# Second columns of the in-projection's norm turned by VectorE squares and one exchange, under three weight blocks summed over the first columns

## The chip, the cores and the metric

The kernel runs on one core of a Trainium2 chip. The metric is the device time of one execution in microseconds (us). A range of 0.2% of this kernel's time, 1.11 us, is about what a measurement can tell from no change.

## The reference

One layer of a decoder trunk on 256 tokens of width 1024, in float32:

```python
h = x + 0.5 * swiglu(rms_norm(x, g1), ...)              # FFN 1, hidden width 2816
u = rms_norm(h, mix_norm)
proj = u @ w_in                                         # 1024 x 5120
q_a, k_a, v_a, q_b, k_b, v_b, g_a, g_b = split(proj)    # 6 x 512, 2 x 1024
y_a = moba(rotary(q_a), rotary(k_a), v_a)               # 256 tokens: plain causal attention
y_b = stick_breaking(q_b, k_b, v_b)
h = h + (sigmoid(g_a) * (y_a @ w_a) + sigmoid(g_b) * (y_b @ w_b)) @ w_out
h = h + 0.5 * swiglu(rms_norm(h, g2), ...)              # FFN 2
out = rms_norm(h, final_norm)
```

## The kernel before

**Matmuls in three passes.** Every float32 operand is split into a high part (`wh`, `uh`, ...) and a rest (`wl`, `ul`, ...), and a product is three matmuls into one PSUM bank (lines 307, 308, 309): high by high, high by rest, rest by high. One `unit` is these three matmuls for one weight tile of 128 x 512 and one token half `t` (128 tokens).

**Weights.** A stream of 376 weight tiles comes from HBM in the order of use, two tiles (512 KB) to a DMA on SP's queue (line 154, `raw`). `Weights.split` makes `wh` on ScalarE (ACT) and `wl` on VectorE (DVE), lines 165/166, or 169/170 where the norm's gain is multiplied in. There are ten pairs of buffers (`WB = 10`): tile i+10 is split when tile i has been used by both token halves. Tiles 132 to 211 belong to the in-projection, eight tiles (the depth 1024 in pieces of 128) to each of ten column blocks of 512: 0 to 2 are q_a, k_a, v_a, 3 to 5 q_b, k_b, v_b, 6 to 9 the gates.

**Order of work.** The orders of TensorE (PE) and SP are written out by hand. `weave` is a list of generators: after every unit a `tick` lets those that are due issue their next step, with waits counted in ticks (the constants `D_...`). The orders of ScalarE, VectorE and GpSimd (POOL) are a scheduler's.

**Norms and turned operands.** The matmul wants the activations with the depth on the partitions. The row scale of the norm, `r` (`rms`), is applied later when a bank is read out; ScalarE takes the squares, VectorE two steps, POOL the Newton steps (lines 354, 360, 361). Columns are turned in one of three ways in `Normed`: `half` turns 512 columns of one token half by four TensorE transposes (line 375, bank `tp_u`) and a split; `moved` turns squares of 32 x 32 on VectorE (line 383) and then moves the squares between partitions by 16 DMAs of 16 KB within SBUF (`exchange`, line 460, half on SP, half on POOL); `moved_both` does that for both token halves with one exchange of 16 DMAs of 32 KB, tiles `zs` (squares) and `zm` (moved). The in-projection's norm (`u`) uses `moved` for the first 512 columns and `half` for the second. The norm of FFN 2 (`z`) uses `moved` for the first columns and `moved_both` for the second.

**FFN 2's start.** Since its second columns come late, `three_blocks` sums three weight blocks over the first columns first (24 units), and then the same three over the second columns (24 units). In the first 24 units token half 1 is 8 units behind half 0, in the second 24 it is 2 behind. Four of the six banks are two pairs of the pool `pr`, two are of the pool `acc`.

**In-projection before.** `project` sums one block over the whole depth: block 0 with half 1 eight units behind, the others two behind. `heads` runs q, k, v in that order; after q and k of the first attention (`rotary`) POOL rotates (`rotate`, lines 740 to 743), and ten ticks later (`D_TURN`) TensorE turns them (`qtpa`, `ktpa`, line 775). Two `lane` generators work through four pairs of heads of each attention, long steps between units of the in-projection: scores `S`, weights turned (`ptp`), values `y_a`; then `z`, its sums over later keys (lines 908 to 910) and `y_b`. What the lanes have not issued when the first columns of the first branch product (`ba`) are done is issued at once (`weave.flush(long=True)`).

Of the kernel before, what the change touches and what calls it, by code (L numbers as in the profile page):

```python
# [21 lines left out]
KD = D // P  # L22
# [8 lines left out]
W_IN = FB * KD + 2 * KF  # L31
# [8 lines left out]
D_TURNED = 3  # L40
# [4 lines left out]
D_TURN = 10  # L45
D_READY = 7
D_NORM = 4
# [3 lines left out]
D_PAIR = (6, 1)  # L51
# [146 lines left out]
def hybrid_layer_kernel(ctx, tc, x, xt, pos, g_final, bgate, wstream, out):  # L198
# [10 lines left out]
    def acc_bank(nm):  # L209
        return psum.tile([P, 512], F32, name=nm, tag="acc", bufs=3)  # L210
# [4 lines left out]
    def two_banks(nm):  # L215
        return psum.tile([P, 1024], F32, name=nm, tag="pr", bufs=2)
# [19 lines left out]
    def gain(i):  # L236
        for n, (lo, hi) in enumerate(((0, FB * KD), (W_IN, W_BR), (W_FFN2, W_FFN2 + FB * KD))):
            if lo <= i < hi:
                k = (i - lo) % KD
                if n == 0 and i < 2 * KD:  # L240
                    k = i // 2
                if n == 2 and i - lo < 3 * KD:
                    k = (i - lo) // 12 * 4 + (i - lo) % 4
                return gk[:, n * KD + k:n * KD + k + 1]
        return None
# [5 lines left out]
    def load_x(queue, k0, k1):  # L251
# [33 lines left out]
                            base=0, pattern=[[0, 4], [-1, P]], channel_multiplier=1)  # L285
# [3 lines left out]
                            base=0, pattern=[[-1, P]], channel_multiplier=1)  # L289
# [11 lines left out]
    weave = Weave()  # L301
# [110 lines left out]
    class Given(Normed):  # L412


        made = [big(f"x{q}{j}") for j in range(2) for q in "hl"]
# [16 lines left out]
    def later(f, *args):  # L432
        f(*args)
        return
        yield

    def lagged(n, lag):

        for k in range(n + lag):
            if k < n:  # L440
                yield 0, k
            if k >= lag:
                yield 1, k - lag
# [18 lines left out]
            if m % len(queues) == len(queues) - 1:  # L462
                yield gap

    def three_blocks(x, base, banks, evac):

        for c in range(2):
            for t, n in lagged(12, 2 if c else KD):
                b, k = divmod(n, 4)
                i = base + c * 12 + n  # L470
                unit(banks(t, b), x[t].blk(c * 4 + k), W.get(i), c == 0 and k == 0, c == 1 and k == 3)
                if t == 1:
                    W.done(i)
                if c == 1 and k == 3:
                    evac(b, t, banks(t, b))


    def ffn(base, xn, nm, on_half, lag, last=False):
# [27 lines left out]
        for b in range(FB):  # L506
            if b == 1:
                W.ahead = AHEAD
            if b == 3 and last:
                ordered.enter_context(tc.manual_schedule())  # L510
            banks = {}
            if b == 0 and lag == 0:
                pairs = [two_banks(f"gu_{nm}{c}") for c in range(2)]
                os = [[pair[:, t * 512:t * 512 + 512] for t in range(2)] for pair in pairs]
                for i in range(2 * KD):
                    k, c = divmod(i, 2)
                    blocks = [xn[t].blk(k) for t in range(2)]
                    if i == 0:
                        keep_warm(os[c], False)
                        unit_halves(os[c], blocks, W.get(base))  # L520
                    else:
                        unit_pair(os[c], blocks, W.get(base + i), k == 0, k == KD - 1)
                    W.done(base + i)

                for c in range(2):
                    for t in range(2):
                        weave.add(later(hidden, c, t, os[c][t]), D_GIVEN[c][t])
            if b == 0 and lag:
                gus = {}

                def gu_bank(t, b):
                    if (t, b) not in gus:
                        if b < 2:

                            pair = two_banks(f"gu_{nm}{b}")
                            gus[0, b], gus[1, b] = pair[:, 0:512], pair[:, 512:1024]
                        else:
                            gus[t, b] = acc_bank(f"gu_{nm}{b}_{t}")
                    return gus[t, b]

                three_blocks(xn, base, gu_bank, lambda b, t, ps: weave.add(later(hidden, b, t, ps), D_PAIR[t] if b < 2 else 0))
            for t, k in lagged(KD, 2) if b > (2 if lag else 1) else ():
                if k == 0:
                    banks[t] = acc_bank(f"gu_{nm}{b}_{t}")
                i = base + b * KD + k
                unit(banks[t], xn[t].blk(k), W.get(i), k == 0, k == KD - 1)
                if t == 1:
                    W.done(i)
                if k == KD - 1:
                    weave.add(later(hidden, b, t, banks[t]))  # L550

        base += FB * KD
        banks = {}
# [45 lines left out]
        for t, c in ((0, 0), (0, 1), (1, 0), (1, 1)) if last else ((0, 0), (1, 0), (0, 1), (1, 1)):  # L599
            pieces = (0, 1) if last and (t, c) == (1, 1) else (None,)  # L600
            for piece in pieces:
                for k in range(head, KF):
                    i = base + 2 * head + c * tail + k - head
# [7 lines left out]
    xn = [Given(t) for t in range(2)]  # L611
# [76 lines left out]
    un = [None, None]  # L688

    def next_norm(dst, nm):  # L690
        both = []

        def on_half(t, c, piece=None):
            def go():
                dst[t].half(c)
                dst[t].rms()
                return
                yield

            if c == 0:  # L700
                dst[t] = Normed(t, nm)
                weave.begin(dst[t].moved(c))
            elif nm == "z":
                weave.add(later(dst[t].rms), D_NORM)
                if t == 0:
                    both.append(Normed.moved_both(c, dst))
                    next(both[0])
                else:
                    weave.begin(both[0])
            else:  # L710
                weave.add(go(), D_NORM)

        return on_half

# [6 lines left out]

    def project(bi, evac):
        banks = {}
        for t, k in lagged(KD, KD if bi == 0 else 2):
            if k == 0:
                banks[t] = acc_bank(f"in{bi}_{t}")
            i = W_IN + bi * KD + k
            unit(banks[t], un[t].blk(k), W.get(i), k == 0, k == KD - 1)
            if t == 1:
                W.done(i)  # L730
            if k == KD - 1:
                evac(t, banks[t])
# [10 lines left out]
        marks["rot"] = g.tensor_add(d3[:, :, 0:16], t1, t2).ins  # L743

    def heads(b0, nm, res, rotary, diagonal):


        for j, which in enumerate("qk"):
# [17 lines left out]
            def turn(which=which, src=src, squares=squares):  # L766
                if rotary:
                    tp = two_banks(f"{which}tp{nm}")
                else:
                    tp = big(f"{which}m{nm}", F32)  # L770
                    yield from exchange(tp, squares, 8, [nc.sync, nc.gpsimd], 1)
                    yield D_LANDED
                for pr in range(4 if rotary else 0):
                    for t in range(2):
                        nc.tensor.transpose(tp[:, pr * 256 + t * P:pr * 256 + (t + 1) * P], src[t][:, pr * P:(pr + 1) * P], ident)
                if which != diagonal:
                    parts = big(f"{which}Th{nm}"), big(f"{which}Tl{nm}")
                    for c in range(2):
                        s = slice(c * 512, c * 512 + 512)
                        if rotary:  # L780
                            split(parts[0][:, s], parts[1][:, s], tp[:, s])
                        else:
                            split(plain(parts[0][:, s]), plain(parts[1][:, s]), slots(tp, 8)[:, c * 4:c * 4 + 4])
                            yield D_PIECE
                    ready = [[q[:, pr * 256:(pr + 1) * 256] for q in parts] for pr in range(4)]
                else:
                    tp4 = slots(tp, 8).rearrange("p (c t) g w -> p c t g w", t=2)
                    for c in range(2):
                        for j in range(2):
                            rows = slice(j * HD, j * HD + HD)  # L790
                            dst = [q[rows].rearrange("p (c j t g w) -> p c j t g w", c=2, j=2, t=2, g=4)[:, :, j] for q in res["bd"][c]]
                            split(dst[0], dst[1], tp4[rows, c * 2:c * 2 + 2])
                            yield D_PIECE
                    ready = [[q[:, pr % 2 * 512:pr % 2 * 512 + 512] for q in res["bd"][pr // 2]] for pr in range(4)]
                yield D_READY if rotary else D_READY - D_PIECE
                res[which] = ready

            if which == diagonal:
                res["bd"] = [(big(f"bdh{nm}{c}"), big(f"bdl{nm}{c}")) for c in range(2)]
                for c in range(2):  # L800
                    for q in res["bd"][c]:
                        for half in range(2):
                            q5 = q[half * HD:(half + 1) * HD].rearrange("p (c j t) -> p c j t", c=2, j=2)
                            nc.gpsimd.memset(q5[:, :, 1 - half, :].bitcast(F32), 0.0)
            project(b0 + j, evac)
            weave.add(turn(), D_TURN if rotary else D_TURNED)

        vs = big(f"vh{nm}"), big(f"vl{nm}")

# [5 lines left out]
            if t == 1:  # L815
                res["v"] = [[q[:, s * 512:(s + 1) * 512] for q in vs] for s in range(2)]

        project(b0 + 2, evac_v)

    def pass3(o, a, b, first, last):  # L820
        for i, (p, q) in enumerate(((0, 0), (0, 1), (1, 0))):
# [100 lines left out]
    a, b, ys = {}, {}, {}  # L922
# [52 lines left out]
    for c in range(2):  # L975
        banks = {}
# [156 lines left out]
```

## Time and profile before

| what | value |
|---|---|
| time, median of 3 runs | 554.25 us (554.15 to 554.33) |
| the profiled execution | 554.34 us, its span from first to last instruction 552.6 us |
| TensorE busy | 545.0 us, 99% of the span, 2490 instructions |
| VectorE, ScalarE, GpSimd busy | 400.6, 338.2 and 78.1 us |
| mean granted TensorE clock | 0.997 |
| DMA queue of SP (q1) | 108.16 MB, 61.3% of the 16 engines' span |

A busy TensorE says little by itself here: matmuls overlap (one of 128 x 512 lasts 0.39 us, and the next starts 0.227 us after it), so a delay is read from the starts, not from the busy time. The rows on which the argument rests stand in the prediction.

### The profile page before, as it was taken

Reading aid. Unit: us, or ns where it says so; the run is one execution under the profiler, and the core shown is the slowest. Engines: PE = TensorE matmul, PEld = TensorE weight load, DVE = VectorE, ACT = ScalarE, POOL = GpSimd, SP = SyncE. Lnnn points to the kernel's source line nnn. Section 1 sums busy time; section 2 is a strip of 40 time slices with the busy share of each in tenths; the row PEclk is TensorE's granted clock in tenths of the full one; section 3 lists DMA queues with packets and bytes.
Section 4 is the critical chain, followed back from the end, with each engine's and each line's share of the span. In section 5 each row is a group of like instructions: output and inputs, shape, how many; then the busy total and the mean of one; then the engine's idle time right before and its main releaser. Section 6 shows DMA issues by size and latency. Waiting matters only on the chain.

```text
span 552.6 us, 7886 instructions
## 1 busy us (share of the span) xinstructions
PE 545.0 (99%) x2490; PEld 449.4 (81%) x2490; DVE 400.6 (72%) x691; ACT 338.2 (61%) x578; POOL 78.1 (14%) x156
## 2 busy tenths in 40 slices
PE   9999999999999999999999999999999999999995
PEld 6888888888888888888888888887888888888884
DVE  5797788766566666889888888777776778655645
ACT  6865666655453767677875774466766566555533
POOL 1410000000003736022022200471000000000000
PEclk9999999999999999999999999999999999999998
DMA  8947776775774676455555464586768766757722
GB/s 283 406 136 238 231 218 206 224 242 180 229 243 157 197 237 213 155 160 182 173 154 175 139 197 151 180 263 215 226 187 251 228 206 210 227 172 246 240 69 76
DMA packets 43722, 112.22 MB, mean 203 GB/s; under 512 B 8352, under 2 KB 17568, under 8 KB 43680
## 3 DMA queue, kind: packets, MB, share of 16 engines
q1 hardware_dynamic: 40992, 108.16, 61.3%
q0 software_dynamic: 2256, 2.89, 2.0%
q10 hardware_dynamic: 432, 0.67, 0.3%
q8 instruction: 19, 0.31, 0.2%
q14 instruction: 23, 0.19, 0.1%
HBM read 102.25 MB, written 1.05 MB: 187 GB/s over the span
## 4 chain that ended last, share of the span: by engine, by line
PE 99%; ACT 0%; DVE 0%; issue 0%; ACTq 0%
PE gu_f L308 13%; PE gu_f L307 13%; PE gu_f L309 13%; PE dn_f L307 7%; PE dn_f L308 7%; PE dn_f L309 7%; PE in L307 7%; PE in L309 7%; PE in L308 7%; PE wo L309 1%; PE wo L307 1%; PE wo L308 1%; PE gu_f L320 1%; PE gu_f L321 1%; PE gu_f L323 1%; PE y_a L822 1%
## 5 line engine op out<-in xcount | busy, mean ns | idle before, releaser
L170 DVE SCALAR_TENSOR_TENSOR wl<-raw,first,wh 128x512 fp32r<-128x512 f32 (+1 forms) x257 | 182.0, 745 | 45.9 <-ACT wh L169 44.9
L169 ACT ACTIVATE wh<-raw,first 128x512 fp32r<-128x512 f32 (+1 forms) x257 | 172.5, 715 | 61.5 <-DMA raw<-in_wstream 34.9
L165 ACT CAST wh<-raw 128x512 fp32r<-128x512 f32 x120 | 70.5, 619 | 63.6 <-DMA raw<-in_wstream 36.0
L166 DVE TENSOR_TENSOR wl<-raw,wh 128x512 fp32r<-128x512 f32 x120 | 78.5, 689 | 39.7 <-ACT wh L165 39.2
L308 PE MATMUL gu_f<-wl,zh 128*128 128x512 f32 x176 | 68.6, 390 | 0.0
L307 PE MATMUL gu_f<-wh,zh 128*128 128x512 f32 x176 | 68.5, 389 | 0.0
L309 PE MATMUL gu_f<-wh,zl 128*128 128x512 f32 x176 | 68.5, 389 | 0.0
L307 PE MATMUL dn_f<-wh,hth_f 128*128 128x512 f32 x172 | 67.1, 390 | 0.0
L309 PE MATMUL dn_f<-wh,htl_f 128*128 128x512 f32 x172 | 66.9, 389 | 0.0
L308 PE MATMUL dn_f<-wl,hth_f 128*128 128x512 f32 x172 | 66.9, 389 | 0.0
L307 PE MATMUL in<-wh,uh 128*128 128x512 f32 x160 | 63.5, 397 | 0.0
L309 PE MATMUL in<-wh,ul 128*128 128x512 f32 x160 | 62.5, 391 | 0.0
L308 PE MATMUL in<-wl,uh 128*128 128x512 f32 x160 | 62.5, 390 | 0.0
L307 PE MATMUL gu_f<-wh,xh 128*128 128x512 f32 x144 | 56.0, 389 | 0.0
L308 PE MATMUL gu_f<-wl,xh 128*128 128x512 f32 x144 | 56.0, 389 | 0.0
L309 PE MATMUL gu_f<-wh,xl 128*128 128x512 f32 x144 | 56.0, 389 | 0.0
L308 PEld LDWEIGHTS gu_f<-wl,zh 128*128 128x128 f32 x176 | 33.0, 188 | 7.3 <-DVE wl L170 0.4
L307 PEld LDWEIGHTS gu_f<-wh,zh 128*128 128x128 f32 x176 | 33.0, 188 | 6.9
L309 PEld LDWEIGHTS gu_f<-wh,zl 128*128 128x128 f32 x176 | 33.0, 188 | 6.8
L307 PEld LDWEIGHTS dn_f<-wh,hth_f 128*128 128x128 f32 x172 | 32.3, 188 | 7.0 <-DVE sh_f L487 0.4
L309 PEld LDWEIGHTS dn_f<-wh,htl_f 128*128 128x128 f32 x172 | 32.3, 188 | 6.8
L308 PEld LDWEIGHTS dn_f<-wl,hth_f 128*128 128x128 f32 x172 | 32.3, 188 | 6.5
(251 smaller groups left out, 780.9 us busy)
## 6 DMA issues: line engine op xcount, KB each, us to landing
raw<-in_wstream SPq DMA_DIRECT2D x185, 512.0 KB, 4.3
hm_f<-hs_f SPq DMA_DIRECT2D x160, 32.0 KB, 3.9
raw<-in_wstream SPq DMA_DIRECT2D x5, 256.0 KB, 4.9
h<-in_x SPq DMA_DIRECT2D x2, 512.0 KB, 8.3
bg<-in_bgate POOLq DMA_DIRECT2D x4, 256.0 KB, 4.7
xin<-in_xt SPq DMA_DIRECT2D x2, 256.0 KB, 6.7
hm_f<-hs_f SPq DMA_DIRECT2D x32, 16.0 KB, 3.1
gB<-in_g_final POOLq DMA_DIRECT2D x1, 512.0 KB, 5.9
```

The costliest lines, as they stand in the source:

```text
L165: self.nc.scalar.copy(hi, raw)
L166: self.nc.vector.tensor_sub(lo, raw, hi.bitcast(F32))
L169: self.nc.scalar.activation(hi[:, s], raw[:, s], AF.Copy, scale=g)
L170: self.nc.vector.scalar_tensor_tensor(lo[:, s], raw[:, s], g, hi[:, s].bitcast(F32), op0=ALU.mult, op1=ALU.subtract)
L307: nc.tensor.matmul(o, ah, wh, start=first, stop=False)
L308: nc.tensor.matmul(o, ah, wl, start=False, stop=False)
L309: nc.tensor.matmul(o, al, wh, start=False, stop=last)
L320: nc.tensor.matmul(o, ah, wh, start=first, stop=False)
L321: nc.tensor.matmul(o, al, wh, start=False, stop=False)
L323: nc.tensor.matmul(o, ah, wl, start=False, stop=last)
L822: nc.tensor.matmul(o, a[p], b[q], start=first and i == 0, stop=last and i == 2, skip_group_check=True)
```

## The change

Norm `u` is now handled like norm `z`: its second columns are turned by `moved_both` (new tiles `us`, `um`), and blocks 0, 1 and 2 of the in-projection (q_a, k_a, v_a) run through `three_blocks`. The stream of weights is put in that order on the host, `gain` finds the right piece of the gain for it, and the banks' helper moves from `ffn` into `three_blocks`. The read-out of q_a, k_a and v_a and the turns of q_a and k_a now hang on the end of each block in the second 24 units.

```diff
-                if n == 2 and i - lo < 3 * KD:
+                if n > 0 and i - lo < 3 * KD:
                     k = (i - lo) // 12 * 4 + (i - lo) % 4
...
-    def three_blocks(x, base, banks, evac):
+    def three_blocks(x, base, nm, evac):
+        made = {}
+        def banks(t, b):
+            if (t, b) not in made:
+                if b < 2:
+                    pair = two_banks(f"{nm}{b}")
+                    made[0, b], made[1, b] = pair[:, 0:512], pair[:, 512:1024]
+                else:
+                    made[t, b] = acc_bank(f"{nm}{b}_{t}")
+            return made[t, b]
...
         def on_half(t, c, piece=None):
-            def go():
-                dst[t].half(c)
-                dst[t].rms()
-                return
-                yield
             if c == 0:
                 dst[t] = Normed(t, nm)
                 weave.begin(dst[t].moved(c))
-            elif nm == "z":
+            else:
                 weave.add(later(dst[t].rms), D_NORM)
                 if t == 0:
                     both.append(Normed.moved_both(c, dst))
                     next(both[0])
                 else:
                     weave.begin(both[0])
-            else:
-                weave.add(go(), D_NORM)
...
-        for t, k in lagged(KD, KD if bi == 0 else 2):
+        for t, k in lagged(KD, 2):
...
-            project(b0 + j, evac)
-            weave.add(turn(), D_TURN if rotary else D_TURNED)
+            steps.append((evac, turn))
+            if not rotary:
+                project(b0 + j, evac)
+                weave.add(turn(), D_TURNED)
...
-        project(b0 + 2, evac_v)
+        if not rotary:
+            project(b0 + 2, evac_v)
+            return
+        steps.append((evac_v, None))
+        def evac_step(b, t, ps):
+            evac, turn = steps[b]
+            evac(t, ps)
+            if t == 1 and turn:
+                weave.add(turn(), D_TURN)
+        three_blocks(un, W_IN, "in", evac_step)
...
-    for b in range(10):
-        st += tiles(a["w_in"][0], b * 512, (b + 1) * 512)
+    blocks = [tiles(a["w_in"][0], b * 512, (b + 1) * 512) for b in range(10)]
+    st += [blocks[b][c * 4 + k] for c in range(2) for b in range(3) for k in range(4)]
+    for b in range(3, 10):
+        st += blocks[b]
```

Three places in the engines' orders show it. The number behind a name is a buffer's.

TensorE before, in the in-projection's first units: token half 0 runs through the eight tiles of block 0, and the second group of four transposes stands between.

```order
L307 MATMUL in0_0_2019<-wh135_1961,uh0_1837 128x512
L308 MATMUL in0_0_2019<-wl135_1962,uh0_1837 128x512
L309 MATMUL in0_0_2019<-wh135_1961,ul0_1838 128x512
L375 MATMUL tp_u11_2048<-ident_109,h1_72 128x128 x4
L307 MATMUL in0_0_2019<-wh136_1974,uh0_1837 128x512
L308 MATMUL in0_0_2019<-wl136_1975,uh0_1837 128x512
L309 MATMUL in0_0_2019<-wh136_1974,ul0_1838 128x512
```

TensorE now, from the tenth unit of the in-projection on (`in2_0` is block 2, token half 0; `in0` block 0, here half 1):

```order
L307 MATMUL in0_2018<-wh132_1909,uh1_1888 128x512
L308 MATMUL in0_2018<-wl132_1910,uh1_1888 128x512
L309 MATMUL in0_2018<-wh132_1909,ul1_1889 128x512
L307 MATMUL in2_0_2090<-wh141_2054,uh0_1837 128x512
L308 MATMUL in2_0_2090<-wl141_2055,uh0_1837 128x512
L309 MATMUL in2_0_2090<-wh141_2054,ul0_1838 128x512
L307 MATMUL in0_2018<-wh133_1920,uh1_1888 128x512
L308 MATMUL in0_2018<-wl133_1921,uh1_1888 128x512
L309 MATMUL in0_2018<-wh133_1920,ul1_1889 128x512
L307 MATMUL in2_0_2090<-wh142_2104,uh0_1837 128x512
L308 MATMUL in2_0_2090<-wl142_2105,uh0_1837 128x512
L309 MATMUL in2_0_2090<-wh142_2104,ul0_1838 128x512
```

The transposes are gone, and tile 142, which takes the buffer of tile 132, is used two units after the last use of tile 132.

GpSimd before, at the end of the Newton steps of token half 1 of norm `u` (`rq1` is its scale for q, `t1_qa0` the rotation of q_a):

```order
L360 TENSOR_SCALAR v_u1_2055<-r_u1_1890,v_u1_2055 128x1
L361 TENSOR_SCALAR r_u1_1890<-v_u1_2055,r_u1_1890 128x1
L756 TENSOR_SCALAR rq1_2018<-r_u1_1890 128x1
L740 TENSOR_TENSOR t1_qa0_2085_2088<-qa0_2085,cos_151 128x128
L741 TENSOR_TENSOR t2_qa0_2085_2089<-qa0_2085,sin_152 128x8x8
```

GpSimd now, at the same place:

```order
L360 TENSOR_SCALAR v_u1_2049<-r_u1_1890,v_u1_2049 128x1
L361 TENSOR_SCALAR r_u1_1890<-v_u1_2049,r_u1_1890 128x1
L750 TENSOR_SCALAR rq1_2015<-r_u1_1890 128x1
L460 DMA um1_1952<-us1_1951 32x256 x8
L732 TENSOR_TENSOR t1_qa0_2223_2226<-qa0_2223,cos_151 128x128
```

POOL's eight DMAs of the new exchange stand behind all Newton steps of both token halves, and ahead of q's rotation.

TensorE before, where the lanes end: the last sums `z3` stand 42 matmuls ahead of the last values `y_b3` (shown are the sums' last two rows, and the rows around the values' first).

```order
L909 MATMUL z3_3304<-sl3_3379,sums_122 128x256
L910 MATMUL z3_3304<-sl3_3379,sums_122 128x2x128
...
L307 MATMUL ba10_3503<-wh213_3385,yah_2397 128x512
L308 MATMUL ba10_3503<-wl213_3386,yah_2397 128x512
L309 MATMUL ba10_3503<-wh213_3385,yal_2398 128x512
L822 MATMUL y_b3_3519<-wwh3_3470,vhb_2719 128x512
```

TensorE now (lines of the changed file are 7 later here):

```order
L916 MATMUL z3_3363<-sl3_3425,sums_122 128x256
L917 MATMUL z3_3363<-sl3_3425,sums_122 128x2x128
...
L307 MATMUL ba10_3507<-wh215_3411,yah_2466 128x512
L308 MATMUL ba10_3507<-wl215_3412,yah_2466 128x512
L309 MATMUL ba10_3507<-wh215_3411,yal_2467 128x512
L829 MATMUL y_b3_3533<-wwh3_3523,vhb_2711 128x512
```

The lanes run about ten units later, `z3` stands just ahead of the first unit of `ba`, and the flush after the first columns of `ba` brings `y_b3` 24 matmuls behind it.

More of the change, by code (lines that the diff above doesn't have):

```diff
@@ L528, in ffn @@
             if b == 0 and lag:
[L529 to L536, printed above, removed]
-                        else:
-                            gus[t, b] = acc_bank(f"gu_{nm}{b}_{t}")
-                    return gus[t, b]
-                three_blocks(xn, base, gu_bank, lambda b, t, ps: weave.add(later(hidden, b, t, ps), D_PAIR[t] if b < 2 else 0))
+                three_blocks(xn, base, f"gu_{nm}",
+                             lambda b, t, ps: weave.add(later(hidden, b, t, ps), D_PAIR[t] if b < 2 else 0))
             for t, k in lagged(KD, 2) if b > (2 if lag else 1) else ():
@@ L709, in on_half @@
                     weave.begin(both[0])
-            else:
-                weave.add(go(), D_NORM)
         return on_half
@@ L745, in heads @@
     def heads(b0, nm, res, rotary, diagonal):
+        steps = []
         for j, which in enumerate("qk"):
```

## Prediction

> **What bounds the kernel now.** I read the page first, then TensorE's rows in time order around the change, then the same start of FFN 2, where the new scheme already runs, and last the engines that feed it.
>
> The page's busy times and its chain that ended last:
>
> ```profile
> PE 545.0 (99%) x2490; PEld 449.4 (81%) x2490; DVE 400.6 (72%) x691; ACT 338.2 (61%) x578; POOL 78.1 (14%) x156
> PEclk9999999999999999999999999999999999999998
> ...
> PE 99%; ACT 0%; DVE 0%; issue 0%; ACTq 0%
> ```
>
> The chain runs through TensorE alone and the clock is full all the time, so the time is TensorE's list of instructions plus its stalls. A change counts here by what it takes from that list, and by the stalls it puts in.
>
> The first group of transposes that goes, in TensorE's rows (start, duration):
>
> ```profile
> 182.86 0.39 PE L309 MATMUL dn_f<-wh,htl_f 128*128 128x512 f32 x1
> 183.09 0.60 PE L375 MATMUL tp_u<-ident,h 128*128 128x128 f32 x4
> 183.44 0.47 PE L307 MATMUL dn_f<-wh,hth_f 128*128 128x512 f32 x1
> 183.75 0.39 PE L308 MATMUL dn_f<-wl,hth_f 128*128 128x512 f32 x1
> ...
> 185.36 0.39 PE L309 MATMUL dn_f<-wh,htl_f 128*128 128x512 f32 x1
> 185.59 0.39 PE L307 MATMUL in<-wh,uh 128*128 128x512 f32 x1
> ```
>
> A matmul starts 0.227 us after the one before (182.86 to 183.09), a unit of three takes 0.68. No start here is late for a wait: the down product, the transposes and the in-projection follow without a hole. So there is no stall in this place for the change to win back.
>
> **The terms.**
>
> *Removed: eight transposes.* From 183.09 to 185.36 there are nine matmul starts, thus eight steps, which at 0.227 take 1.81 us; they took 2.27. One group costs 0.46 us (0.35 for itself, 0.08 for the slow matmul behind it, the rest in the next ones). Two groups: **-0.91 us**. Nothing hid them. The splits that read their banks (one cast on ACT, one subtraction on VectorE per group) are replaced by the same splits from `um`; the two VectorE squares added take the 0.70 us of this row each, beside TensorE:
>
> ```profile
> 367.50 0.70 DVE L396 STREAM_TRANSPOSE zs<-h 128x512 f32<-128x512 f32 x1
> ```
>
> *Moved: the units themselves.* They are the same 480 matmul triples; another order costs nothing where the operands are there. Two operands are new in that: the weights of tile 142, and the second columns.
>
> *Added wait 1: the buffer of tile 142.* FFN 2's start shows it, with the same lags and ten buffers. TensorE, ACT and VectorE at the thirteenth unit there:
>
> ```profile
> 365.85 0.39 PE L307 MATMUL gu_f<-wh,zh 128*128 128x512 f32 x1
> ...
> 372.65 0.39 PE L307 MATMUL gu_f<-wh,zh 128*128 128x512 f32 x1
> ...
> 374.01 0.39 PE L307 MATMUL gu_f<-wh,zh 128*128 128x512 f32 x1
> 374.42 0.50 PE L308 MATMUL gu_f<-wl,zh 128*128 128x512 f32 x1
> 374.75 0.39 PE L309 MATMUL gu_f<-wh,zl 128*128 128x512 f32 x1
> 372.85 0.73 ACT L169 ACTIVATE wh<-raw,first 128x512 fp32r<-128x512 f32 x1 [2.64 <-PE gu_f L309]
> 373.61 0.75 DVE L170 SCALAR_TENSOR_TENSOR wl<-raw,first,wh 128x512 fp32r<-128x512 f32 x1 [2.57 <-ACT wh L169]
> ```
>
> The tenth unit (half 1 on the first tile) ends at 372.8, ACT then fills the buffer, VectorE ends its part at 374.36, and the second matmul of the thirteenth unit (36 matmuls after 365.85) starts at 374.42 where 374.24 was due; with the next one (0.33 after it) the hole is 0.18 + 0.10, and 0.04 in the rest: **+0.32 us**. The in-projection has one unit between the same two events, and ACT and VectorE are through with tiles 140 and 141 by then, so I take the same value; between 0 (if block 0's split were faster, which no row shows) and 1.0 (VectorE one operation late).
>
> *Added wait 2: the second columns.* They are due at the first unit over them. TensorE reaches the in-projection 0.46 earlier than at 185.59, at 185.13; 24 units of 0.68 and the 0.32 make it 201.77. The high part `uh` is due then, the rest `ul` two matmuls later, at 202.23. When do they come? The exchange's sixteen DMAs go half over SP, half over POOL. SP's eight wait only for VectorE's squares and for `raw` loads around them; POOL's eight stand behind the Newton steps, here of token half 1 and, for their spread, the same eight operations of half 0 (first and last):
>
> ```profile
> 183.29 0.21 POOL L354 TENSOR_SCALAR v_u<-v_u 128x1 f32<-128x1 f32 x1 [1.01 <-DVE v_u L352]
> ...
> 187.28 0.66 POOL L756 TENSOR_SCALAR rq<-r_u 128x1 f32<-128x1 f32 x1
> 188.73 0.21 POOL L354 TENSOR_SCALAR v_u<-v_u 128x1 f32<-128x1 f32 x1 [0.79 <-DVE v_u L352]
> ...
> 193.22 0.74 POOL L756 TENSOR_SCALAR rq<-r_u 128x1 f32<-128x1 f32 x1
> ```
>
> They take 4.65 us there and 5.23 here. Their start stays at 188.7: the residual that the squares' sum needs comes 0.5 earlier, but a VectorE square (0.70) is now queued ahead of that sum's next step. So POOL issues its first DMA between 193.4 and 194.0. Issue and flight are read from the exchange of norm `z` (first four rows; then its last two DMAs on POOL) and of the first columns, `uq` (likewise):
>
> ```profile
> L460 POOL DMA_DIRECT2D zm<-zs x8: 496/534/589, 368.9 to 373.7; - x8
> L338 ACT CAST zh<-zm x2: 611/613/615, 379.3 to 379.8; 128x512 fp32r<-128x512 f32 x2
> L339 DVE TENSOR_TENSOR zl<-zm,zh x2: 687/690/692, 380.2 to 380.8; 128x512 fp32r<-128x512 f32 x2
> DMA to landing us min/median/max: 3.8/4.7/5.7
> L460 POOL DMA_DIRECT2D zm<-zs x2: 527/534/542, 372.9 to 373.7; - x2
> DMA to landing us min/median/max: 4.7/4.7/4.7
> L460 POOL DMA_DIRECT2D uq<-uq x16: 496/498/704, 172.8 to 181.8; - x16
> DMA to landing us min/median/max: 1.6/3.3/4.2
> L460 POOL DMA_DIRECT2D uq<-uq x2: 496/497/498, 181.3 to 181.8; - x2
> DMA to landing us min/median/max: 3.3/3.5/3.7
> ```
>
> Seven issues of 0.53 put the last one at 197.1 to 197.7. Its flight is anything from 1.6 to 5.7 us, landing between 198.7 and 203.4. The nearest rows are the last two of `uq` (the same columns' statistics, the same queue, 3.3 to 3.7); since the last two of `zm` took longer still, I take the upper of them: 197.2 + 3.7 = 200.9. ACT then needs 0.1 + 0.61 for `uh`, VectorE starts 0.28 after that cast's end (379.3 + 0.61 to 380.2) and needs 0.69: `uh` is there 0.7 and `ul` 1.7 after the landing. So a landing up to 200.5 costs nothing, mine costs **+0.35 us**, the latest 2.9.
>
> The Trainium skill, "DMA: Bandwidth & Descriptors", section on the anatomy of one DMA on the GpSimd path, gives a fixed 2.0 us plus bytes over 436e3 for one DMA, which for 32 KB is an estimate of 2.1 us. By that the landing would be 199.3, the wait 0 and the time 553.75; the trace shows 3.8 as the least of `zm`, so I keep the rows' value.
>
> *Moved: the lanes, ten units later.* Their distances in units stay, except at the end. There the chain from the last sums to `y_b3`:
>
> ```profile
> 314.04 0.28 PE L910 MATMUL z<-sl,sums 128*128 128x256 f32 x1
> 314.41 0.81 ACT L912 ACTIVATE w<-z 128x768 f32<-128x768 f32 x1 [0.36 <-PE z L910]
> 315.29 1.78 POOL L880 TENSOR_SCALAR_AFFINE_SELECT w<-w 128x256 f32<-128x256 f32 x2 [4.02 <-ACT w L912]
> 317.11 0.56 DVE L338 CAST wwh<-w 128x768 fp32r<-128x768 f32 x1 [0.30 <-POOL w L880]
> 317.78 0.96 DVE L339 TENSOR_TENSOR wwl<-w,wwh 128x768 fp32r<-128x768 f32 x1
> 323.43 0.39 PE L822 MATMUL y_b<-wwh,vhb 128*128 128x512 f32 x1
> ```
>
> From 314.3 to 318.74 it takes 4.4 us. The new order leaves 24 matmuls, 5.4 us, so 1.0 is left over: **0**, covered by `ba`'s eight units. If VectorE had two weight splits in between it would be 0.4. One more place is tight, ScalarE's queue at the fourth pair of `S`: the squares of k_b come through an exchange there too, and what ACT does for them now stands ahead of the exponentials of `S3`. Before, VectorE's last part of `p3` ended just ahead of its transposes:
>
> ```profile
> 261.17 0.27 DVE L864 TENSOR_SCALAR p<-p,st 128x128 f32<-128x128 f32 x1
> 261.98 0.81 PE L868 MATMUL ptp<-ident,p 128*128 128x128 f32 x6
> L338 ACT CAST kThb<-kmb x2: 609/613/617, 264.2 to 264.7; 128x512 fp32r<-128x512 f32 x2
> ```
>
> It had 0.5 us to spare; the two casts now ahead are 1.1, and the transposes come no earlier after `S3` than before. I take 0, with up to 1.0 for the range.
>
> *The sum.* The profiled execution is 554.34 (span 552.6 and 1.74 around it): 554.34 - 0.91 + 0.32 + 0.35 + 0 = 554.10. It lies 0.09 over the median of the runs, so against these it is **554.0 us**, a change of -0.24 us.
>
> **The rivals.**
>
> *The exchange is hidden.* If POOL's last DMA lands by 200.5, that is if its flight is under 3.3 us (the median of `uq`), only wait 1 is left: 554.25 - 0.59 = 553.66. For it: half of `uq` flew shorter. Against: all of `zm` flew longer, at the same stage of the weights' loading.
>
> *The exchange is late, and the kernel is slower.* The place is the 25th unit of the in-projection, the mechanism POOL's queue, Newton steps ahead of the DMAs. It decides from a landing at 202.25 on, where the stall is 1.7 us and eats both the 0.59 won and 1.11 more; at the latest landing, 203.4, the stall is 2.85 and the time 556.5. For it: a flight of 5.1 us from 197.2 is enough, and `zm` had 4.7 in the median; `zm`'s POOL part was issued between Newton steps, this one behind them. Against: no last DMA of either exchange flew longer than 4.7, and the last of `uq` stayed under 3.8.
>
> *VectorE holds up POOL's descriptors.* If each of the eight issues waited for a weight split of VectorE (0.75 in the row of wait 1), the landing would be 6 us later and the time about 560. In the rows an issue took 0.53 beside VectorE's splits and 0.50 without, so 0.24 in all. The Trainium skill, "SBUF — State Buffer", section on the two separate sides, has that rule: a DMA issued from GpSimd can't get its descriptors written while VectorE holds the shared port. By it the change would lose clearly; the trace's 0.03 per issue does not bear it out.
>
> *A lane comes late* (the fourth `S` pair, or `y_b3`): at most 1.4 in sum on top of 554.0, thus 555.4, which is just slower.
>
> *Clearly faster* would need more than the 0.91 us taken away, since no stall is there to be won.
>
> **How the numbers follow.** Forecast, a small wait for the exchange, 0.42; hidden, 0.34; exchange late 0.13; descriptors 0.02; a lane late enough to be slower 0.06; something I don't see, 0.03 faster. The first two both lie within 0.2% (1.11 us): same 0.76, slower 0.21, faster 0.03. The range goes from -0.91 alone (553.3) to stalls of 2.4 us in place of the 0.67 taken (555.7); a tenth of the late landing's and a little of the rest lie above it.
>
> **What would show it.** In the changed trace, no row of line 375 with `tp_u`; TensorE's first unit of the in-projection 0.4 to 0.5 us earlier; a hole of about 0.3 at the thirteenth unit, with the wait on VectorE's `wl`; at the 25th unit a start later than due, with `uh` or `ul` from `um` as releaser, and POOL's `um` issues from 193.4 on; `ptp` of the fourth pair and `y_b3` without a hole. I am wrong if the 25th unit waits more than 1.7 us, or if a hole stands in the lanes, or if `um`'s second half leaves POOL before 193.

## The result and the profile after

The changed kernel takes 557.99 us (median of 6 runs, 557.66 to 558.38) against 554.29 us before on the same chip (6 runs, 553.88 to 554.49): ratio 1.0068, 95% interval 1.0055 to 1.0081, thus 3.7 us slower. The prediction was 554.0 us, in a range of 553.3 to 555.7. The eight transposes are gone and TensorE reaches the in-projection 0.54 us earlier; behind that stand 4.8 us of new stalls.

The page of the changed kernel, busy times and the chain that ended last:

```profile
PE 545.7 (98%) x2482; PEld 448.8 (81%) x2482; DVE 401.3 (72%) x693; ACT 340.8 (61%) x578; POOL 81.0 (15%) x164
PEclk9999999999999999999999999999999999999998
...
PE 86%; DVE 5%; DMA 4%; ACT 2%; issue 1%; POOL 1%; SPq 0%; ACTq 0%; DVEq 0%
```

Eight instructions fewer, and yet TensorE is busy 0.7 us longer; the clock row hasn't moved. What has changed is the chain: 99% TensorE before, 86% now, with pieces over VectorE, DMAs and ScalarE. The table of TensorE's waits says where (engine, line, what was waited for: sum, times, longest):

```profile
PE ptp L875 <- DVE p L871: 1.4, 1, 1.4
PE in L307 <- ACT ka L753: 1.1, 1, 1.1
PE warm L298 <- DVE zeros L277: 1.1, 1, 1.1
PE in L307 <- ACT qa L751: 0.8, 1, 0.8
```

Only the row of `warm`, at the kernel's start, was there before. The stalls in TensorE's own rows (start, duration), from the first unit of the in-projection to the late transposes:

```profile
185.05 0.39 PE L307 MATMUL in<-wh,uh 128*128 128x512 f32 x1
...
193.21 0.39 PE L307 MATMUL in<-wh,uh 128*128 128x512 f32 x1
193.61 0.51 PE L308 MATMUL in<-wl,uh 128*128 128x512 f32 x1
193.95 0.40 PE L309 MATMUL in<-wh,ul 128*128 128x512 f32 x1
...
201.49 0.39 PE L309 MATMUL in<-wh,ul 128*128 128x512 f32 x1
201.82 0.50 PE L307 MATMUL in<-wh,uh 128*128 128x512 f32 x1
202.16 0.39 PE L308 MATMUL in<-wl,uh 128*128 128x512 f32 x1
202.55 0.51 PE L309 MATMUL in<-wh,ul 128*128 128x512 f32 x1
202.89 0.40 PE L307 MATMUL in<-wh,uh 128*128 128x512 f32 x1
...
205.44 0.39 PE L309 MATMUL in<-wh,ul 128*128 128x512 f32 x1
206.67 0.50 PE L307 MATMUL in<-wh,uh 128*128 128x512 f32 x1 [0.84 <-ACT qa L751]
207.00 0.40 PE L308 MATMUL in<-wl,uh 128*128 128x512 f32 x1
...
212.03 0.39 PE L309 MATMUL in<-wh,ul 128*128 128x512 f32 x1
213.49 0.51 PE L307 MATMUL in<-wh,uh 128*128 128x512 f32 x1 [1.07 <-ACT ka L753]
213.84 0.40 PE L308 MATMUL in<-wl,uh 128*128 128x512 f32 x1
...
257.65 0.39 PE L309 MATMUL in<-wh,ul 128*128 128x512 f32 x1
259.45 0.85 PE L875 MATMUL ptp<-ident,p 128*128 128x128 f32 x6 [1.41 <-DVE p L871]
```

Read from start to start against the 0.227 of an undisturbed step: 0.29 us at the 13th unit (193.21 to 193.95, two steps), 0.49 at the 25th (four steps from 201.49), 1.11 at the 30th (205.44 to 207.00), 1.35 at the 38th (212.03 to 213.84), and 1.57 ahead of the third pair's weight transposes (257.65 to 259.45; the expectations have 1.61, with the slower steps behind it). That makes 4.81; minus the 0.91 of the transposes it is +3.90, where the two profiled executions differ by 4.04 (558.38 and 554.34).

The two small holes are the two waits that were predicted. The exchange behind the second (its DMAs and splits):

```profile
L460 POOL DMA_DIRECT2D um<-us x8: 496/496/556, 193.1 to 196.6; - x8
L338 ACT CAST uh<-um x2: 615/618/621, 201.1 to 201.7; 128x512 fp32r<-128x512 f32 x2
DMA to landing us min/median/max: 3.3/4.1/5.1
```

The three large holes, 4.03 us, were in no term of the sum.

### The profile page after: what moved, and what is told of

Read it like the earlier page. It is cut to its first block, busy times and chain, and to the rows that moved or that the text cites. A ratio compares the mean times of both kernels' runs of the same rounds, so it can differ in the third digit from the quotient of the medians.

```text
span 556.7 us, 7893 instructions
## 1 busy us (share of the span) xinstructions
PE 545.7 (98%) x2482; PEld 448.8 (81%) x2482; DVE 401.3 (72%) x693; ACT 340.8 (61%) x578; POOL 81.0 (15%) x164
## 3 DMA queue, kind: packets, MB, share of 16 engines
HBM read 102.25 MB, written 1.05 MB: 186 GB/s over the span
## 4 chain that ended last, share of the span: by engine, by line
PE 86%; DVE 5%; DMA 4%; ACT 2%; issue 1%; POOL 1%; SPq 0%; ACTq 0%; DVEq 0%
PE gu_f L308 13%; PE gu_f L309 13%; PE gu_f L307 13%; PE dn_f L309 6%; PE dn_f L307 6%; PE dn_f L308 6%; PE in L307 4%; PE in L309 4%; PE in L308 4%; DMA raw<-in_wstream 3%; DVE wl L170 2%; PE wo L309 1%; PE wo L307 1%; PE wo L308 1%; PE gu_f L320 1%; PE gu_f L321 1%
```

## The experiments

The kernels differ in their starts by up to 1.1 us from execution to execution, so beside the time stands the stage in which the change works, from the first unit of the in-projection to the first of `ba` (both read in TensorE's rows). "Pair" is the hole ahead of the weight transposes `ptp` of the third or, behind a comma, the fourth pair. Times are medians; before was 554.3 to 554.4 beside each.

| kernel | time | stage | 13th | 25th | 30th | 38th | pair | other holes |
|---|---|---|---|---|---|---|---|---|
| before | 554.29 | 133.76 | 0 | 0 | 0 | 0 | 0 | |
| changed | 557.99 | 138.27 | 0.29 | 0.49 | 1.11 | 1.35 | 1.57 | |
| e1, read-outs deferred | 558.28 | 136.81 | 0.29 | 0.39 | 0 | 0 | 2.81 | |
| e2, TensorE transposes, `pr` | 561.48 | 141.29 | 0.29 | 0 | 1.11 | 1.05 | 1.02 | 2.54 and 1.44 at the 5th |
| e9, TensorE transposes, `acc` | 558.57 | 138.19 | 0.29 | 0 | 1.75 | 1.05 | 1.26 | |
| e3, lanes 6 units earlier | 558.75 | 138.89 | 0.29 | 0.53 | 1.11 | 1.81 | 0 | 0.65 `ktpa`, 0.85 `vlb` |
| e4, eleven buffers | 560.67 | 140.70 | 0 | 1.44 | 1.11 | 1.86 | 0.99, 0.97 | 0.77 `y_a` |
| e11, q_b's splits held back | 558.88 | 138.82 | 0.29 | 0.82 | 1.11 | 1.61 | 0, 1.27 | 0.21 `y_a` |
| e8, e1 + lanes 3 units earlier | 554.77 | 135.88 | 0.29 | 0.76 | 0 | 0 | 1.45 | |
| e6, e1 + e11 | 554.41 | 133.97 | 0.29 | 0.38 | 0 | 0 | 0 | |
| e7, e6 + Newton steps, lag 7 | 553.50 | 133.20 | 0 | 0 | 0 | 0 | 0 | |
| e10, e7 + lag 7 in FFN 2 | 552.88 | 133.17 | 0 | 0 | 0 | 0 | 0 | |

Each hole is read in one profiled execution, and the kernels with late edits show how far a hole differs from one execution to the next. Up to the 38th unit e3 and e11 have the changed kernel's instructions in the changed kernel's order on every engine, and yet the hole at the 25th unit is 0.49, 0.53 and 0.82, and that at the 38th 1.35, 1.81 and 1.61. The 13th and the 30th are the same in all three. Differences of this size at the 25th and 38th unit can't be put down to an edit.

**e1: the read-outs deferred.** In the changed kernel a block's bank is read out at once when its half is summed. FFN 2's start, which the scheme was taken from, puts its read-outs of the first two blocks off by `D_PAIR` (6 units for half 0, 1 for half 1).

```diff
-        three_blocks(un, W_IN, "in", evac_step)
+        def put(b, t, ps):
+            if b < 2:
+                weave.add(later(evac_step, b, t, ps), D_PAIR[t])
+            else:
+                evac_step(b, t, ps)
+        three_blocks(un, W_IN, "in", put)
```

> The changed kernel (557.99 us) with one edit: the read-outs of blocks 0 and 1 (q_a, k_a) are put off by 6 units for token half 0 and by 1 for half 1, as the start of FFN 2 does, so that both come after the last matmul into their pair of banks. Theory A (a pair of banks is one tile: the read-out of half 0 makes the next matmul into half 1 of the same pair wait, 1.11 us at the 30th unit and 1.35 at the 38th): both holes go, 557.99 - 2.46 = 555.5 us; the 0.29 at the 13th unit, the 0.49 at the 25th and the 1.61 ahead of the third pair's weight transposes stay. Rival B (ScalarE is simply behind with its weight splits after the late exchange): the holes stay or turn up a few units later as waits on wh, 558.0 us.

Theory A holds: the holes at the 30th and 38th unit are gone. Why they were there can be seen without any time, in TensorE's instructions of the changed kernel with their waits; `in0` is the tile of two banks that holds block 0 for both halves:

```
L309 MATMUL in0_2018<-wh147_2154,ul0_1838 128x512
L307 MATMUL in0_2018<-wh145_2136,uh1_1888 128x512 [waits Activation_49]
```

The first row ends half 0's sum. The second goes into half 1's bank, and its operands were used before; what it waits for is ScalarE's read-out of half 0 (the semaphore's count is the one that this read-out sets), since both banks are one tile to the program and the read-out was issued between the two. From the end of the last matmul (205.44 + 0.39) to the end of the read-out TensorE, whose order is fixed, stands still. The Trainium skill, "PSUM — Partial Sum Buffer", section on bank collisions, has matmuls and reads in different banks run side by side; by that rule this wait was the program's own and none of the chip's, and e1, in whose program it doesn't stand, shows no hole there.

The time did not follow the expected 555.5, though: the third pair's hole grew from 1.57 to 2.81, and the start took 0.73 more in the profiled execution (first unit at 185.78, not 185.05). Two of the four runs, 558.57 and 559.14, had a mean granted clock of 0.994 and 0.993, the two others 0.997. ScalarE's and TensorE's rows of e1 at the hole:

```profile
244.07 0.62 ACT L338 CAST bdhb<-qmb 64x512 fp32r<-64x512 f32 x1 [3.99 <-DMA qmb<-qsb]
...
245.73 0.47 ACT L873 ACTIVATE p<-S,st 128x256 f32<-128x256 f32 x1
...
254.50 0.48 ACT L873 ACTIVATE p<-S,st 128x256 f32<-128x256 f32 x1 [0.64 <-DVE st L868]
259.36 0.84 PE L881 MATMUL ptp<-ident,p 128*128 128x128 f32 x6 [2.65 <-DVE p L877]
```

TensorE came to this place at 256.33, in the changed kernel at 257.65, but the transposes start at 259.36 here and at 259.45 there: what had been saved ahead of the pair was waited out at it. The pair's chain did not come earlier with TensorE. ScalarE sat still for 3.99 us in front of q_b's turned squares, with the exponentials of pair 1 behind them, which had been ready since VectorE's last reduction at 242.7.

**e3, e8, e11 and e6: the lanes.** What stands ahead of the third pair's scaling (`p2`) is a matter of VectorE's order. Before the change both scalings of `p2` stood ahead of q_b's four `bdlb`; in the changed kernel, ten units later against q_b, all four and `pl1` stand ahead of them. VectorE's rows of the changed kernel:

```profile
251.70 0.70 DVE L859 TENSOR_TENSOR S<-S,mask_a 128x512 f32<-128x512 f32 x1
252.43 0.69 DVE L339 TENSOR_TENSOR bdlb<-qmb,bdhb 64x512 fp32r<-64x512 f32 x1
...
255.45 0.68 DVE L339 TENSOR_TENSOR bdlb<-qmb,bdhb 64x512 fp32r<-64x512 f32 x1
...
256.72 0.16 DVE L869 RECIPROCAL st<-st 128x4 f32<-128x4 f32 x1
256.91 0.69 DVE L339 TENSOR_TENSOR bdlb<-qmb,bdhb 64x512 fp32r<-64x512 f32 x1
257.63 0.96 DVE L339 TENSOR_TENSOR pl<-ptp,ph 128x768 fp32r<-128x768 f32 x1
258.50 1.00 DVE L871 TENSOR_SCALAR p<-p,st 128x256 f32<-128x256 f32 x4
```

The reciprocal is done at 256.88, the scaling starts 1.6 us later, behind a split of q_b and one of `pl1`, and that is the hole. Four edits test it. e3 moves the lanes, and nothing else, six units earlier:

```diff
-D_TURN = 10
+D_TURN = 4
```

> The changed kernel with D_TURN 4 in place of 10: q_a and k_a are turned six units (4.1 us) earlier, and the lanes with their steps start that much earlier. Theory D (the hole of 1.61 us ahead of the third pair's weight transposes is VectorE's and ScalarE's queue: the lane stands so late that its steps meet the splits of q_b's turned squares): that hole goes, 557.99 - 1.6 = 556.4 us, the holes at the 30th and 38th unit stay. Rival E (the lane's chain is too long for its distance in units wherever it stands): a hole of 1 to 2 us ahead of one of the weight transposes stays, 558.0 us.

The hole at the third pair went, as theory D has it, but the time did not: TensorE now came to `ktpa` before POOL had rotated k_a (0.65), and to a bank that `vlb` had not been read from (0.85). These two took back nearly all of the 1.57. e8 starts from e1 and moves only k_a's turn and the lanes, by three units:

```diff
-                weave.add(turn(), D_TURN)
+                weave.add(turn(), 7 if b else D_TURN)
```

> The kernel with deferred read-outs, with k_a turned three units earlier (7 after its end in place of 10), so that the lanes stand three units earlier and nothing else is touched. Theory D (the lanes' place against q_b's and k_b's turns makes the hole): the order on ScalarE puts the exponentials of pair 1 ahead of bdhb there, and the hole of 2.81 us falls under 1.5, the run 556.5 to 557.2 us. Rival E (chain too long): the hole stays at 2 us or more, 558.3 us.

2.81 became 1.45 (in an execution of 556.07 us, the longest of its runs; the median is 554.77). e11 and e6 leave the lanes where they are and hold q_b's four splits back, until the third pair's last exponential on ScalarE and its scaling on VectorE:

```diff
-                            split(dst[0], dst[1], tp4[rows, c * 2:c * 2 + 2])
+                            while "p2" not in marks:
+                                yield 1
+                            with tc.issue_after(marks["e2"]), tc.issue_after(marks["p2"]):
+                                split(dst[0], dst[1], tp4[rows, c * 2:c * 2 + 2])
```

> The kernel with deferred read-outs (558.28 us, 136.81 us from the first unit of the in-projection to the first of ba) with one more edit: the four splits of q_b's turned squares (bdhb on ScalarE, bdlb on VectorE) may stand on their engines only behind the third pair's exponentials and its scaling. Theory D (the hole ahead of the third pair's weight transposes, 2.81 us there, is a queue: ScalarE waits at bdhb for an exchange with the exponentials of pair 1 behind it, and VectorE does the four bdlb ahead of the scaling): the hole shrinks to 0.5 us or less, the stage takes 134.0 to 134.5 us and the run 555.5 to 556.0. Rival E (the pair's own chain is too long for its distance): the hole stays at 2 us or more, 557.5 to 558.5 us.

This shows that it is the queue: with the read-outs deferred as in e1, the hole of 2.81 is gone, with the pair's own steps unchanged. VectorE and TensorE of e6:

```profile
252.71 0.18 DVE L878 RECIPROCAL st<-st 128x4 f32<-128x4 f32 x1 [1.19 <-ACT p L876]
252.92 1.01 DVE L880 TENSOR_SCALAR p<-p,st 128x256 f32<-128x256 f32 x4
255.69 0.39 PE L309 MATMUL in<-wh,ul 128*128 128x512 f32 x1
255.92 0.82 PE L884 MATMUL ptp<-ident,p 128*128 128x128 f32 x6
```

Scaled at 253.93, used at 255.92, without a late start. The time is 554.41 (10 runs, 553.55 to 557.23; ratio 1.0001, 0.9986 to 1.0015). The same edit on the changed kernel without e1's:

> The changed kernel (557.99 us) with the mend of q_b's splits alone: they may stand only behind the third pair's exponentials and scaling; the read-outs are not deferred. If the four holes are separate, the hole of 1.61 us ahead of the third pair's weight transposes goes and the others stay: stage 136.7 us, run 556.4 us. If the hole there came from the read-outs' delay, it stays, about 558 us.

A miss. The third pair's hole went as expected, but one of 1.27 opened at the fourth, and 558.88 is no gain. VectorE worked almost without a pause from 255.20 on, and q_b's splits now stood in this stretch (256.34 to 262.03, in the changed kernel 248.88 to 257.60). The fourth pair's scaling ended at 273.42, 1.0 us later than there, while TensorE came to that place 1.0 us earlier. That the splits pushed it back is the likely reading; no run isolates it. Either way the holes in the lanes are not separate things, since closing one opened another. The 0.82 and 1.61 at the 25th and 38th unit lie ahead of the edit and are no effect of it.

**e2 and e9: the norm part undone.** Both keep the three blocks and turn the second columns by TensorE again; e9 takes the transposes' banks from `acc` instead of `pr`.

```diff
+        def both_ways(t, c):
+            dst[t].half(c)
+            dst[t].rms()
...
+            elif nm == "u":
+                weave.add(later(both_ways, t, c), D_NORM)
```

> The changed kernel with its norm part undone: the second columns of norm u are turned by eight TensorE transposes again, three blocks summed over the first columns stay. Theory A (the loss is in the banks' read-outs and in the lanes, not in the exchange): the transposes cost 0.91 us again, the hole of 0.49 us at the 25th unit goes, the holes at the 30th and 38th unit and at the weight transposes stay, 557.99 + 0.91 - 0.49 = 558.4 us. Rival C (the late exchange sets off the later waits): the holes after the 25th unit shrink too, about 555.5 to 556.

> The changed kernel with its norm part undone (eight TensorE transposes for the second columns), but their banks taken from the pool acc, so that they don't wait for the two pairs of pr that the three blocks hold (that made 2.46 us of stall and some 1.7 us of slow matmuls behind it in the run with pr). Expected of the norm part by itself: plus 0.91 for the transposes, minus 0.49 for the hole at the 25th unit, which goes; the holes at the 30th and 38th unit and at the weight transposes stay (1.1, 1.1 and 1.0 in the run with pr): 557.2 to 558.4 us. If the late exchange is behind the later holes, these are gone and the run takes 555.5 us.

e2 was badly made: the three blocks hold both pairs of `pr`, so block 1 waited for a transposes' bank (2.54 us by the rows, and 1.44 in the slow matmuls behind it). e9 is the fair one, 558.57: without the exchange there is no hole at the 25th unit, and the three large ones are still there (1.75, 1.05, 1.26). So the loss belongs to the three blocks and to what they shift, not to VectorE's squares or the exchange.

**e4: eleven buffers.**

```diff
-WB = 10
+WB = 11
```

> The changed kernel with eleven pairs of weight buffers in place of ten. If the hole of 0.29 us at the 13th unit is the wait for the buffer of tile 142 and nothing else, it goes here and so does the one of 0.32 us at the same unit of FFN 2's start; the rest stays: 557.99 - 0.6 = 557.4 us. Rival: the splits run further ahead and crowd ScalarE and VectorE elsewhere (read-outs, lanes), 558 us or more.

The hole at the 13th unit went, here and in FFN 2, so it is the buffer of tile 142. The rival had the time right, but not the way to it. The exchange of `um` landed at 201.33 in place of 200.62, because POOL's Newton steps ended later and its DMAs left from 193.86 on, not from 193.12; the last one flew 4.0 us in both kernels. Why the steps took longer in this execution is open. ScalarE waited for the landing with the later splits behind, and the hole at the 25th unit grew to 1.44:

```profile
L460 POOL DMA_DIRECT2D um<-us x8: 496/496/552, 193.9 to 197.3; - x8
201.86 1.14 ACT L338 CAST uh<-um 128x512 fp32r<-128x512 f32 x2 [4.22 <-DMA raw<-in_wstream]
202.53 0.50 PE L307 MATMUL in<-wh,uh 128*128 128x512 f32 x1 [0.90 <-ACT uh L338]
```

Besides it, the holes of 0.97 at the fourth pair and 0.77 at `y_a` are new; no run isolates their cause.

**e7 and e10: all mends together.** e7 adds two to e6: the Newton steps of half 1 may stand on POOL only behind the first of its eight exchange DMAs, and half 1 is seven units behind in the first 24 units, not eight, so that tile 132's buffer comes free one unit earlier.

```diff
+            with tc.issue_after(marks["um"]):
...
-            for t, n in lagged(12, 2 if c else KD):
+            for t, n in lagged(12, 2 if c else lag):
```

> All mends together: read-outs deferred, q_b's splits behind the third pair, the Newton steps of token half 1 behind the first of POOL's eight exchange DMAs, and half 1 seven units behind in the first 24 units in place of eight. If the hole at the 25th unit comes from POOL's Newton steps ahead of the DMAs, the last landing is at 198 us or before and that hole (0.39 to 0.49 us) goes; if the hole at the 13th unit is the buffer of tile 142, which now comes free one unit earlier, that one (0.29) goes too. The stage takes 133.0 to 133.6 us (133.76 before the change), the run 553.5 to 554.3 us, against 554.3 to 554.4 before the change. Rival: the engines beside TensorE are so full that a hole that is closed opens elsewhere, 555.5 us or more.

POOL's rows of e7, the line of the exchange's casts, and TensorE's table of waits:

```profile
188.61 2.04 POOL L468 DMA_DIRECT2D um<-us  x4 [0.47 <-DMA raw<-in_wstream]
190.67 0.24 POOL L358 TENSOR_SCALAR v_u<-v_u 128x1 f32<-128x1 f32 x1
...
193.93 0.55 POOL L468 DMA_DIRECT2D um<-us  x1
```

```profile
L338 ACT CAST uh<-um x2: 617/619/621, 198.2 to 198.8; 128x512 fp32r<-128x512 f32 x2
```

```profile
PE warm L298 <- DVE zeros L277: 1.1, 1, 1.1
```

POOL's last DMA leaves at 193.93, not 196.6, `uh` is cast from 198.2 and not from 201.1, and no hole is left in the stage. 553.50 us (12 runs) against 554.38: ratio 0.9982, interval 0.9971 to 0.9992. The 0.88 gained agree with the 0.91 of the transposes, though the interval is wide beside them (0.4 to 1.6 us). e10 gives FFN 2's start the same lag of seven:

> The kernel with all mends (553.5 us), with half 1 seven units behind in the first 24 units of FFN 2's start as well. If the hole at the thirteenth unit there (0.29 us in every kernel so far but the one with eleven buffers) is the same buffer wait, it goes: 553.2 us. Rival: half 1's first columns of norm z come too late for a unit less, and a hole of 0.3 to 0.7 us opens at the eighth unit: 553.5 to 554.

The hole there is gone, and nothing opened. 552.88 us (8 runs) against 554.37, ratio 0.9971, interval 0.9961 to 0.9982: the fastest version, 1.5 us under the kernel before. In the profiled executions the stretch from `ba` to the end is 0.33 shorter than in e7 (232.98 and 233.31), which is the hole; the other 0.3 of the medians' difference is within the intervals.

## Why the prediction was wrong

- *Removed transposes, -0.91.* Right: e7, which has no hole but those of before, is 0.88 faster, within its interval.
- *Wait 1, +0.32.* Right in place, cause and size: 0.29, and gone with one more buffer or with half 1 one unit nearer.
- *Wait 2, +0.35.* Right in place and cause, in size partly by luck. POOL's last DMA left at 196.6 (197.2 predicted) and flew 4.0 us, not 3.7, so two errors offset each other in the landing, 200.62 where 200.9 was predicted. ScalarE then started 0.5 after it, not 0.1, for a reason that no run shows, and the hole was 0.49; in the six executions with the same instructions up to there (the changed kernel, e1, e3, e6, e8, e11) it was 0.38 to 0.82. Newton steps ahead of POOL's DMAs were the reason, as said: e7 put them behind.
- *Moved units, "another order costs nothing where the operands are there".* This step failed. Two operands were looked at, weights and second columns; the third thing that a matmul needs, its bank, was not. A read-out between two matmuls into one tile cost 1.11 and 1.35 us. The pattern to compare with was in the kernel: FFN 2's read-outs have their `D_PAIR`, the in-projection's have not, and only weights were compared between the two starts.
- *Moved lanes, 0.* This step failed too, by 1.57 us. Their distances among themselves stay, but not those to q_b's and k_b's turns, and the two places that were worked out (`y_b3`, the fourth pair) were not the one that became late. The third pair's chain now had q_b's splits between its steps on VectorE's queue (252.43, 255.45 and 256.91). The two steps that failed make 4.03 of the 4.28 us by which the profiled execution, 558.38, lies above the sum's 554.10.
- *The rivals.* Slower was the outcome, but not by the mechanism that was given (the exchange). "A lane comes late" had 0.06 and a limit of 1.4; none of them had the read-outs. VectorE did not hold up POOL's descriptors: their issues took 0.496 us in the median, as `uq`'s did. By its own test ("or if a hole stands in the lanes") the prediction named what would make it wrong.

## What to carry to other kernels

When a scheme is moved from one place of a program to another, list everything that a matmul waits for, operands and the bank, and compare the constants around the scheme at its old place one by one; a tile of several banks is one thing to the program's waits. Shifting work by units against a neighbour changes the order on the queues of engines that look half idle (72% and 61% here), and it is that order, at the exact place, that decides, so check each consumer's chain, not the tightest of before. Judge mends together: e1 removed 2.46 us of holes and gained nothing until the next hole behind it was closed as well. And read a hole in more than one execution before its size is called an effect: the same instructions gave 1.35 us once and 1.81 another time.

## What the runs showed of the hardware

The clock can fall within a stall of 2.3 us. In e2 TensorE stood from 188.80 to 191.10; windows of that stretch (columns: TensorE busy, granted clock, DMA share, GB/s), and rows behind it:

```profile
189.50:190.00 0.50, 0.00 (x0) 1.00 0.50 115
190.50:191.00 0.50, 0.00 (x0) 0.78 0.91 360
191.50:193.50 2.00, 2.00 (x6) 0.50 0.43 107
```

```profile
192.12 0.63 PE L309 MATMUL in<-wh,ul 128*128 128x512 f32 x1
192.55 0.63 PE L307 MATMUL in<-wh,uh 128*128 128x512 f32 x1
```

By the second row the clock fell at about 190.8, 2.0 us after TensorE's last work. The matmuls start 0.43 apart at clock 0.50: from the first start behind the stall to the eighth it is 3.13 us (191.10 to 194.23), where it is 1.69 in the kernel before (188.67 to 190.36), so 1.44 came on top of the stall. In e1's profile a stall of 2.65 us left the clock at 1.00. The Trainium skill, "TensorE: Matmul & The Clock Gate", Part 1, gives 426.7 ns from start to start for the cold array, which agrees, and one idle window of about 3.4 us as what it takes; here 2.0 us without work were enough once, and a longer stall did nothing in another run.
